# Down projection of a three-product float32r FFN: two of three matmuls joined over a whole PSUM bank, and weight sums moved from Pool to accumulating DMAs

## The chip, the cores and the metric

The kernel runs on one core of one Trainium2 chip, as one program. The metric is the device time of one execution in microseconds (us), as the median of several runs. The profile is that of one execution; its engines are PE (TensorE, matmul; PEld is its weight load), DVE (VectorE), ACT (ScalarE), POOL (GpSimd) and SP (SyncE, which here only issues DMAs).

## The reference

One layer of an encoder for 512 tokens of 2048 features, all in float32: a norm, a combined projection, two mixers, an output projection with residual, then a SwiGLU network (FFN) with residual and a last norm. The change touches the FFN alone, and there the last matrix product, the down projection by `w_down`:

```python
D_MODEL, SEQ, D_FF = 2048, 512, 5632

def reference(x, ..., w_gate_up, w_down, final_norm_w):
    ...                                   # norm, input projection, mixers
    x = x + jnp.einsum('bse,ed->bsd', mixed, w_out[l])
    h2 = _rmsnorm(x, ffn_norm_w[l])
    g, u = jnp.split(jnp.einsum('bsd,df->bsf', h2, w_gate_up[l]), 2, axis=-1)
    x = x + jnp.einsum('bsf,fd->bsd', jax.nn.silu(g) * u, w_down[l])
    return _rmsnorm(x, final_norm_w)
```

## The kernel before

**Numbers.** A float32 operand is split into two float32r parts: `hi`, a copy rounded by ACT (L931 for weights), and `lo`, the rest, by a DVE subtraction (L128, the method `sub`). A product of two such operands is three matmuls into the same PSUM region: hi\*bh, hi\*bl, lo\*bh (L180 to L182, in `mm3`; b is the activation).

**Units.** The FFN's matrix products are cut into units, each by a Winograd scheme with seven products in place of eight. A unit has two blocks of 128 output features as rows, 2048 (in the last block of hidden features 1536) of the summed dimension, and all 512 tokens in two halves of H = 256. It loads two raw weight tiles of 128x2048 (upper: `a11`, `a12`; lower: `a21`, `a22`). Products are taken in the order 1, 2, 4, 5, 6, 3, 7 and called p1 to p7 here. One product is eight tiles of 128 features times three matmuls of 256 columns into the first half of one PSUM bank. A product's activations are its "forms" (sums of quarters of the activation, already split), held in SBUF slots of 128x512 as [bh | bl], 256 columns each.

**Sums of weights.** The scheme needs a21 += a22, a11 -= a21, a12 += a11 and a22 += a11 on the raw tiles (L907 to L923, L128, L131). With the flag `dma` set, three of them are DMAs that accumulate, issued by Pool (L907): the first when the lower tile is loaded, the others ahead of p5's weights. Without it two are adds on Pool (L909), ahead of p4's and p6's weights, and a22 += a11 is a DVE add (L131). The subtraction a11 -= a21 is on DVE in both.

**Evictions.** After p1, p5, p6 and p7 ACT copies 256 columns out of PSUM (L962, L969 are among them), after p2 and p3 and twice after p7 DVE adds 256 columns (L131, L134). In the down projection two results of 128x512 are then added to `x1d` in DRAM by accumulating DMAs issued by Pool (L1015).

**The order.** `Stream` runs the products ("steps") of all units one after another. Units 0 to 43 are gate and up; 44 to 51 and 52 to 59 are the down projection over the first two blocks of hidden features (2048 each), 60 to 67 the last block (1536) with residual and norm. Most units run singly, a unit's p3 and p7 being put behind the next unit's p1 and p2. At the borders of the blocks two units are zipped product by product: 44 with 45, 50 with 51, 52 with 53, 58 with 59, 60 with 61. So a form is wanted twice in a row there, and a pair needs four raw tiles, which are all there are (`RAWB` = 4). A unit's raw tiles are loaded when the splits of p3 and p7 of the unit two before are done.

Weights are split four steps ahead of their product (five `hi` and `lo` buffers). The forms of a block come from `hfd` in DRAM, 56 slots of 256 KB, and take the place of the block before: `reload` (L1319) puts a product's eight loads on SP's queue one to three steps after the last unit of a block has used that product. SP's queue is in order, raw weights and forms together.

Slots of 128x512 for temporaries come from the pool `tp`, nine of them (`TPN`). In gate and up the forms of the result are made in such slots (ACT copy L1187 and DVE subtraction) and stored to `hfd`.

The functions that the change touches, and what calls them:

Of the kernel before, what the change touches and what calls it, by code (L numbers as in the profile page):

```python
# [7 lines left out]
F32 = mybir.dt.float32  # L8
# [7 lines left out]
P = 128  # L16
# [6 lines left out]
B12 = 4  # L23
# [14 lines left out]
# Products, by phase, whose forms are spilled unsplit.  # L38
PLAIN = [(), (1, 2, 4), (), ()]
RAWB, HLB = 4, 5  # L40
SPN, TPN, HPN = 39, 9, 19

# [9 lines left out]
class K:  # L52
# [18 lines left out]

    def bank(self, tag):
        return self.ps.tile([P, T], F32, tag=tag, name=self.nm(tag), bufs=self.banks[tag])
# [21 lines left out]
    def rec_constants(self):  # L95
        """The masks of the recurrence's levels, to DRAM, and the lower bounds."""
# [14 lines left out]
        # Lower bounds: softmax over the layers, its running sum, less its first term.  # L111
# [24 lines left out]
    def split(self, hi, lo, src):  # L136
        """src = hi + lo, each of float32r's twelve bits."""
        self.nc.scalar.copy(hi, src)  # L138
        self.sub(lo, src, hi.bitcast(F32))
# [32 lines left out]
    def weights(self, dram, n=DM, pieces=1):  # L172
        """Chunks of [P, <=QW] of a weight row: loaded, split."""
# [10 lines left out]
    def gemm(self, ws, act, tick=None):  # L184
        """act: pairs of a K tile and its parts, in the order of their use."""
# [10 lines left out]
    def rstd_steps(self, sq, n, tn=T, plus=None, keep=None, over=None, fill=lambda n: None):  # L196
        """From squares summed over all but the partitions: 1/rms as columns, then as rows.

        plus: columns of further sums; keep: takes the columns of these; over: columns that
        the result is divided by.  # L200
        """
# [31 lines left out]
    def stationary(self, Kt, B):  # L233
        """kf in the first halves of blocks of 2B, kb in the second."""
# [5 lines left out]
    def recurrence(self, q, Kt, T1, V, res):  # L240
        """q: slot, Kt: [kf|kb], T1: [ff|fb], V: by token tile. Leaves o (in PSUM) in res."""
# [73 lines left out]
def body(tc, xT, small, wi, wp, wo, wg, wd, out):  # L315
    with ExitStack() as ctx:
# [3 lines left out]
        k.tp = k.pool(ctx, "tp", TPN)  # L320
# [26 lines left out]
        forms, rho = out_proj(k, xT, mhl, wo, x1d, fd)  # L347
        with tc.manual_schedule(engines=by_hand):
# [3 lines left out]
def start(k, xT, wi, wp, vd, zd):  # L352
    """x by features, times the gains, and its forms but t3; its 1/rms.

    Meanwhile v of the first four heads, by tokens, and the rest of the first head.
    """
# [141 lines left out]
def load_b12(k, xT):  # L498
    """The second half of the tokens of the first half of x's features."""
# [10 lines left out]
def conv(k, j, u, y):  # L510
    """y: the taps of channels j on u"""
# [7 lines left out]
def stream(k, hT, F, rest, xT, wp, gd, qd, md, zd):  # L519
    """The gates of all heads, some of the q and most of the conv, by units of two tiles."""  # L520
# [52 lines left out]
    # The step after which t3 makes way for b12.  # L573
# [30 lines left out]
def heads(k, ctx, hT, w0, z0, wi, wp, gd, qd, vd, md):  # L604
# [16 lines left out]
    def segment():  # L621
        """A share of the pending recurrence: it has PARTS steps."""
# [8 lines left out]
    def values_mm(w):  # L631
        """v of two heads, by tokens."""
# [782 lines left out]
```

## Time and profile before

| | |
|---|---|
| median of three runs | 2364.51 us (2364.26 to 2366.21) |
| span of the profiled execution | 2367.5 us |
| PE busy | 2329.9 us, 98% of the span, 17226 matmuls |
| DVE busy | 1752.6 us, 74% |
| ACT busy | 1061.4 us, 45% |
| Pool busy | 342.2 us, 14% |
| gate and up (units 0 to 43) | until about 1900 us |
| down projection of the first two blocks (units 44 to 59) | about 1900 to 2220 us |

The page gives busy times as shares of the span. They are averages over stages; what sets the time of a stage is read from the tables of stretches and from PE's own timeline, in which a gap of PE is followed by the name of what ended it. The profiled span is 3.0 us above the median of the runs.

### The profile page before, as it was taken

What the parts mean: (1) busy time and instruction counts of PE and PEld (TensorE: products, weight loads), DVE (VectorE), ACT (ScalarE), POOL (GpSimd) and SP (SyncE); (2) the same over time, 40 slices, a digit from 0 to 9 for tenths busy, and PEclk for the clock granted to TensorE, in tenths of its full rate; (3) what the DMA queues carried; (4) which work ended last, traced back from release to release, by engine and by line L of the source; (5) the groups of instructions that cost most, each with busy time, mean ns of one, the idle gap of its engine ahead of it and who ended that gap; (6) DMA issues with size and microseconds to landing.
All of it is one profiled execution on the core that took longest, in us unless ns stands there. A gap on an engine that the chain in (4) does not pass through costs nothing.

```text
span 2367.5 us, 42647 instructions
## 1 busy us (share of the span) xinstructions
PE 2329.9 (98%) x17226; PEld 2219.7 (94%) x17226; DVE 1752.6 (74%) x2457; ACT 1061.4 (45%) x1593; POOL 342.2 (14%) x300
## 2 busy tenths in 40 slices
PE   8999999999999999999999999999999989999997
PEld 8999999888888788899999999999999989999997
DVE  8867768766667756687777777777777798777777
ACT  7444445333333333444444445454545544444453
POOL 0231110000000100121111111111111033333210
PEclk9999999999999999999999999999999999999998
DMA  6377776221222455567887878788888884975984
GB/s 232 130 213 203 192 190 221 103 77 66 81 81 72 143 173 205 182 227 219 215 228 204 226 212 238 221 243 220 236 228 230 239 285 129 290 226 138 294 235 135
DMA packets 143684, 454.63 MB, mean 192 GB/s; under 512 B 15744, under 2 KB 31872, under 8 KB 118400
## 3 DMA queue, kind: packets, MB, share of 16 engines
q1 hardware_dynamic: 110528, 349.09, 41.3%
q0 software_dynamic: 30640, 100.68, 22.7%
q8 instruction: 135, 2.21, 0.4%
q10 hardware_dynamic: 2320, 2.15, 0.3%
q14 instruction: 61, 0.50, 0.1%
HBM read 291.75 MB, written 71.50 MB: 153 GB/s over the span
## 4 chain that ended last, share of the span: by engine, by line
PE 91%; DMA 5%; DVE 2%; issue 1%; ACT 1%; POOL 0%; POOLq 0%; SPq 0%; DVEq 0%; ACTq 0%
PE g L180 22%; PE g L181 22%; PE g L182 22%; PE r L180 6%; PE r L182 6%; PE r L181 6%; PE r L268 2%; DMA raw<-wd 1%; PE r L311 1%; DVE lo L128 1%; DMA raw<-wg 1%; DMA s<-fd 1%; DMA s<-hfd 1%; PE r L283 1%; DMA raw<-raw 1%
## 5 line engine op out<-in xcount | busy, mean ns | idle before, releaser
L180 PE MATMUL g<-s,hi 128*128 128x256 f32 (+1 forms) x3912 | 1194.7, 305 | 5.7 <-ACT s L962 4.1
L181 PE MATMUL g<-s,hi 128*128 128x256 f32 (+1 forms) x3912 | 1180.5, 302 | 0.0
L182 PE MATMUL g<-s,lo 128*128 128x256 f32 (+1 forms) x3912 | 1179.8, 302 | 0.0
L128 DVE TENSOR_TENSOR lo<-raw,hi 128x1024 fp32r<-128x1024 f32 (+2 forms) x689 | 869.3, 1268 | 329.8 <-ACT hi L931 236.3
L931 ACT CAST hi<-raw 128x1024 fp32r<-128x1024 f32 (+1 forms) x581 | 597.1, 1028 | 837.6 <-PE g L181 336.1
L180 PEld LDWEIGHTS g<-s,hi 128*128 128x128 f32 x3912 | 749.6, 192 | 34.3 <-ACT s L962 4.9
L181 PEld LDWEIGHTS g<-s,hi 128*128 128x128 f32 x3912 | 749.7, 192 | 27.4 <-issue 3.8
L182 PEld LDWEIGHTS g<-s,lo 128*128 128x128 f32 x3912 | 749.1, 191 | 27.3 <-issue 0.2
L180 PE MATMUL r<-s,hi 128*128 128x256 f32 x1296 | 368.4, 284 | 7.5 <-DVE s L131 7.5
L182 PE MATMUL r<-s,lo 128*128 128x256 f32 x1296 | 368.5, 284 | 3.6 <-DVE lo L128 3.6
L181 PE MATMUL r<-s,hi 128*128 128x256 f32 x1296 | 368.1, 284 | 0.0
L907 POOL DMA_DIRECT2D raw<-raw x173 | 150.9, 986 | 967.9 <-ACT hi L931 779.8
L180 PEld LDWEIGHTS r<-s,hi 128*128 128x128 f32 x1296 | 250.3, 193 | 8.7 <-issue 4.4
L182 PEld LDWEIGHTS r<-s,lo 128*128 128x128 f32 x1296 | 250.2, 193 | 4.2 <-DVE lo L128 4.2
L181 PEld LDWEIGHTS r<-s,hi 128*128 128x128 f32 x1296 | 250.2, 193 | 0.0
L909 POOL TENSOR_TENSOR raw<-raw 128x1024 f32<-128x1024 f32 (+1 forms) x48 | 129.2, 2696 | 506.4 <-DVE s L128 188.6
L134 DVE TENSOR_TENSOR s<-s,s 128x512 f32<-128x512 f32 (+1 forms) x258 | 177.1, 693 | 5.6
L138 ACT CAST hi<-raw 128x1024 fp32r<-128x1024 f32 (+1 forms) x108 | 105.1, 984 | 163.8 <-PE g L181 151.1
L128 DVE TENSOR_TENSOR s<-s,s 128x256 fp32r<-128x256 f32 (+2 forms) x302 | 129.6, 458 | 6.5 <-ACT s L138 5.0
L128 DVE TENSOR_TENSOR raw<-raw,raw 128x1024 f32<-128x1024 f32 (+1 forms) x83 | 105.5, 1271 | 4.2 <-DMA raw<-raw 4.2
L131 DVE TENSOR_TENSOR s<-s,r 128x256 f32<-128x256 f32 x166 | 68.8, 415 | 37.2 <-PE r L182 35.9
L219 POOL TENSOR_TENSOR rc<-ms,mhalf 128x4 f32<-128x4 f32 (+1 forms) x13 | 12.7, 979 | 472.4 <-DVE ms L216 472.4
(138 smaller groups left out, 1617.4 us busy)
## 6 DMA issues: line engine op xcount, KB each, us to landing
raw<-wg SPq DMA_DIRECT2D x88, 1024.0 KB, 5.3
raw<-raw POOLq DMA_DIRECT2D x157, 512.0 KB, 7.0
raw<-wp SPq DMA_DIRECT2D x56, 1024.0 KB, 5.2
hfd<-s SPq DMA_DIRECT2D x130, 256.0 KB, 5.7
s<-hfd SPq DMA_DIRECT2D x130, 256.0 KB, 5.4
raw<-wd SPq DMA_DIRECT2D x32, 1024.0 KB, 5.9
raw<-wo SPq DMA_DIRECT2D x16, 1024.0 KB, 5.3
raw<-wd SPq DMA_DIRECT2D x16, 768.0 KB, 4.9
```

The costliest lines, as they stand in the source:

```text
L128: self.nc.vector.tensor_tensor(out=out, in0=a, in1=b, op=ALU.subtract)
L131: self.nc.vector.tensor_tensor(out=out, in0=a, in1=b, op=ALU.add)
L134: self.nc.vector.tensor_tensor(out=out, in0=a, in1=b, op=ALU.mult)
L138: self.nc.scalar.copy(hi, src)
L180: mm(out, ahi, bhi, start=start, stop=False, **kw)
L181: mm(out, ahi, blo, start=False, stop=False, **kw)
L182: mm(out, alo, bhi, start=False, stop=stop, **kw)
L268: nc.tensor.matmul(ps[:, g * P:(g + 1) * P], kc[:, g * P:(g + 1) * P], vap(Qt, g * P, dims), start=True, stop=True)
L283: nc.tensor.matmul(ps[:, j * 256:(j + 1) * 256], Kt[:, d, s * P:(s + 1) * P], Qt[:, 1 - d, tq:tq + 256], start=True, stop=True)
L907: pool.dma_start(out=out, in_=a, accum_op=ALU.add)
L909: pool.tensor_tensor(out=out, in0=out, in1=a, op=ALU.add)
L931: k.nc.scalar.copy(hi, src)
```

## The change

It has four parts.

1. *Two matmuls in one.* The units 44 to 59 are of a new class `Wide`. The weights `hi` meet the whole slot [bh | bl] in one matmul of 512 columns over a whole bank: hi\*bh lands in the first half, hi\*bl in the second. Then lo\*bh, 256 columns, is added to the second half. The wanted product is the sum of the two halves. So each eviction takes both halves (512 columns) into "pair" tiles of 128x2x2x256, four of them (`DPF`), and at the end of each result one more DVE add of 512 columns joins the halves.
2. *Sums by DMA.* `Down` is built with `dma` set: three accumulating DMAs per unit (L916 after) where Pool's two adds and DVE's add into a22 were.
3. *Stores.* The accumulating store to `x1d` (L1072 after) reads every other 256 columns of a pair tile, so its pieces are 1 KB where they were 2 KB.
4. *Room.* The pool `tp` is closed before the FFN and opened again as `tf` with eight slots instead of nine; the program's scratch for descriptors of DMAs is set to 2048 where the default stood, which gives SBUF room back; a form's entry in `F` holds the whole slot as a third item. Docstrings went, so line numbers move.

The core of the diff:

```diff
+TPF, DPF = 8, 4
+RING = 2048
+    def pair(self):
+        return self.tp.tile([P, 2, 2, H], F32, tag="d", name=self.nm("d"), bufs=DPF)
...
         forms, rho = out_proj(k, xT, mhl, wo, x1d, fd)
+        tctx.close()
+        k.tp = k.pool(tctx, "tf", TPF, side="right", reuse_waits="tile")
...
+class Wide(Unit):
+    def product(self, p, w):
...
+        for j in range(self.nj):
+            s = slice(j * P, (j + 1) * P)
+            f = self.F[FORMS[p], j][2]
+            mm(ps, w[0][:, s], f, start=start and j == 0, stop=False, skip_group_check=True)
+            mm(ps[:, H:], w[1][:, s], f[:, :H], start=False, stop=stop and j == self.nj - 1,
+               skip_group_check=True)
+
+    def post(self, p):
+        k = self.k
+        copy = k.nc.scalar.copy
+        two = lambda ps: vap(ps, 0, [[H, 2], [1, H]])
+        if p == 1:
+            self.G = k.pair()
+            copy(self.G[:, 0], two(self.b))
+        elif p == 2:
+            k.add(self.G[:, 0], self.G[:, 0], two(self.a))
+        elif p == 5:
+            self.W = k.pair()
+            copy(self.W[:, 1], two(self.d))
+        elif p == 6:
+            copy(self.G[:, 1], two(self.b))
+        elif p == 3:
+            G = self.G
+            k.add(G[:, 1], G[:, 1], two(self.d))
+            k.add(G[:, :, 0], G[:, :, 0], G[:, :, 1])
+        elif p == 7:
+            W = self.W
+            copy(W[:, 0], two(self.b))
+            k.add(W[:, 1], W[:, 1], W[:, 0])
+            k.add(W[:, 0], W[:, 0], two(self.e))
+            k.add(W[:, :, 0], W[:, :, 0], W[:, :, 1])
...
-class Down(Unit):
+class Down(Wide):
     def post(self, p, add0, add1):
         super().post(p)
         if p == 7:
-            for out, t in ((add0, self.g), (add1, self.lower())):
-                self.k.nc.gpsimd.dma_start(out=out, in_=t, accum_op=ALU.add)
+            for out, t in ((add0, self.G), (add1, self.W)):
+                self.k.nc.gpsimd.dma_start(out=out, in_=t[:, :, 0], accum_op=ALU.add)
...
-            make.append((lambda b=b, c=c, d=d: Down(k, (wd[d, :, c], wd[d + 8, :, c]), F[1 + b]),
+            make.append((lambda b=b, c=c, d=d: Down(k, (wd[d, :, c], wd[d + 8, :, c]), F[1 + b], True),
...
-    nc = _bacc.Bacc("TRN2", target_bir_lowering=False, num_devices=1)
+    nc = _bacc.Bacc("TRN2", target_bir_lowering=False, num_devices=1,
+                    dynamic_dma_scratch_size=RING)
```

PE, in one product of the first down units. The names are output bank, then form and weight part; `s` is a form's slot. Before:

```order
L180 MATMUL g_2581_20119<-s_2516_19720,hi_2565_19990 128x256
L181 MATMUL g_2581_20119<-s_2516_19720,hi_2565_19990 128x256
L182 MATMUL g_2581_20119<-s_2516_19720,lo_2569_20020 128x256
L180 MATMUL g_2581_20119<-s_2517_19722,hi_2565_19990 128x256
L181 MATMUL g_2581_20119<-s_2517_19722,hi_2565_19990 128x256
L182 MATMUL g_2581_20119<-s_2517_19722,lo_2569_20020 128x256
```

And after:

```order
L1021 MATMUL g_2579_20074<-s_2516_19726,hi_2564_19979 128x512
L1022 MATMUL g_2579_20074<-s_2516_19726,lo_2567_20000 128x256
L1021 MATMUL g_2579_20074<-s_2517_19728,hi_2564_19979 128x512
L1022 MATMUL g_2579_20074<-s_2517_19728,lo_2567_20000 128x256
L1021 MATMUL g_2579_20074<-s_2518_19730,hi_2564_19979 128x512
L1022 MATMUL g_2579_20074<-s_2518_19730,lo_2567_20000 128x256
```

Three instructions per tile became two; the columns per tile, 768, stay the same.

DVE in the first stretch, units 44 and 45 (raw 2504 and 2511 are the upper and lower weights of 44, raw 2508 and 2514 those of 45; `r` is the bank of p2). Before:

```order
L128 TENSOR_TENSOR raw_2504_19595<-raw_2504_19595,raw_2511_19676 128x1024
L128 TENSOR_TENSOR lo_2569_20020<-raw_2511_19676,hi_2565_19990 128x1024
L128 TENSOR_TENSOR raw_2508_19637<-raw_2508_19637,raw_2514_19715 128x1024
L131 TENSOR_TENSOR s_2561_19959<-s_2561_19959,r_2568_19995 128x256
L128 TENSOR_TENSOR lo_2572_20051<-raw_2514_19715,hi_2570_20023 128x1024
L131 TENSOR_TENSOR s_2566_19992<-s_2566_19992,r_2571_20026 128x256
L128 TENSOR_TENSOR lo_2575_20082<-raw_2504_19595,hi_2573_20054 128x1024
L128 TENSOR_TENSOR lo_2578_20112<-raw_2508_19637,hi_2576_20085 128x1024
L131 TENSOR_TENSOR raw_2511_19676<-raw_2511_19676,raw_2504_19595 128x1024
```

And after:

```order
L134 TENSOR_TENSOR raw_2504_19599<-raw_2504_19599,raw_2511_19680 128x1024
L134 TENSOR_TENSOR lo_2567_20000<-raw_2511_19680,hi_2564_19979 128x1024
L134 TENSOR_TENSOR raw_2508_19641<-raw_2508_19641,raw_2514_19720 128x1024
L137 TENSOR_TENSOR d_2561_19955<-d_2561_19955,r_2566_19983 128x512
L134 TENSOR_TENSOR lo_2570_20025<-raw_2514_19720,hi_2568_20005 128x1024
L137 TENSOR_TENSOR d_2565_19981<-d_2565_19981,r_2569_20008 128x512
L134 TENSOR_TENSOR lo_2573_20047<-raw_2504_19599,hi_2571_20027 128x1024
L134 TENSOR_TENSOR lo_2576_20068<-raw_2508_19641,hi_2574_20049 128x1024
L134 TENSOR_TENSOR lo_2580_20091<-raw_2504_19599,hi_2577_20070 128x1024
```

The order stays, with the adds out of PSUM twice as wide and the add into a lower raw tile gone; the two subtractions of raw tiles now follow an accumulating DMA where they followed a Pool add.

Pool around units 52 and 53. Before:

```order
L909 TENSOR_TENSOR raw_2758_21614<-raw_2758_21614 128x1024
L1015 DMA x1d_83<-s_2706_21317 128x512
L1015 DMA x1d_83<-s_2711_21350 128x512
L909 TENSOR_TENSOR raw_2761_21645<-raw_2761_21645 128x1024
L1015 DMA x1d_83<-s_2773_21695 128x512
L1015 DMA x1d_83<-s_2776_21725 128x512
L909 TENSOR_TENSOR raw_2751_21550<-raw_2751_21550 128x1024
L909 TENSOR_TENSOR raw_2755_21583<-raw_2755_21583 128x1024
```

And after:

```order
L916 DMA raw_2752_21216<-raw_2752_21216 128x1024
L1072 DMA x1d_83<-d_2700_20983 256x1x256
L1072 DMA x1d_83<-d_2704_21009 256x1x256
L916 DMA raw_2755_21240<-raw_2755_21240 128x1024
L1072 DMA x1d_83<-d_2745_21171 256x1x256
L1072 DMA x1d_83<-d_2750_21196 256x1x256
L916 DMA raw_2743_21167<-raw_2743_21167 128x1024
L916 DMA raw_2752_21216<-raw_2743_21167 128x1024
L916 DMA raw_2748_21192<-raw_2748_21192 128x1024
L916 DMA raw_2755_21240<-raw_2748_21192 128x1024
```

The two adds per unit are three DMAs, of which the last two stand together; the stores to `x1d` keep their places between them.

## Rows read from the trace of the kernel before

**Rows 1.** The page: busy us, share of span, instructions of each engine.

```profile
PE 2329.9 (98%) x17226; PEld 2219.7 (94%) x17226; DVE 1752.6 (74%) x2457; ACT 1061.4 (45%) x1593; POOL 342.2 (14%) x300
```

**Rows 2.** Stretches, single units: window, us, busy by engine, PEclk, DMA share, GB/s.

```profile
1930.00:2020.00 90.00, 89.93 (x750) 89.72 (x748) 71.14 (x68) 38.87 (x54) 33.66 (x19) 1.00 0.59 171
...
2110.00:2180.00 70.00, 70.00 (x586) 70.00 (x585) 53.06 (x45) 28.35 (x37) 23.34 (x13) 1.00 0.50 133
```

**Rows 3.** The same view: 512-column matmuls of an earlier stage, then 256-column ones.

```profile
900.00:950.00 50.00, 50.00 (x222) 41.39 (x221) 28.20 (x47) 16.55 (x28) 0.00 (x0) 1.00 0.58 198
...
1950.00:2000.00 50.00, 50.00 (x419) 50.00 (x419) 39.67 (x36) 20.54 (x27) 15.60 (x9) 1.00 0.55 136
```

**Rows 4.** PE's timeline, units 44, 45 (start, us; bracket: idle before); the stretch.

```profile
1900.04 0.28 PE L180 MATMUL r<-s,hi 128*128 128x256 f32 x1
...
1902.23 0.39 PE L182 MATMUL r<-s,lo 128*128 128x256 f32 x1 [1.79 <-DVE lo L128]
...
1906.28 0.38 PE L182 MATMUL r<-s,lo 128*128 128x256 f32 x1 [0.91 <-DVE lo L128]
...
1917.42 0.36 PE L180 MATMUL r<-s,hi 128*128 128x256 f32 x1 [4.22 <-DVE s L131]
...
1890.00:1921.00 31.00, 23.02 (x173) 22.04 (x172) 29.58 (x31) 13.63 (x21) 10.70 (x4) 0.95 0.99 375
```

**Rows 5.** Timeline of DVE and of Pool in the same stretch.

```profile
1898.77 3.41 DVE L128 TENSOR_TENSOR lo<-raw,hi 128x1024 fp32r<-128x1024 f32 x1
...
1905.00 1.22 DVE L128 TENSOR_TENSOR lo<-raw,hi 128x1024 fp32r<-128x1024 f32 x1
...
1895.89 5.20 POOL L909 TENSOR_TENSOR raw<-raw 128x1024 f32<-128x1024 f32 x2 [30.96 <-DVE lo L128]
```

**Rows 6.** Stretches with sums by DMA in gate/up, one with a store; Pool's issues.

```profile
1526.00:1535.00 9.00, 9.00 (x78) 9.00 (x77) 6.41 (x11) 4.35 (x6) 1.89 (x3) 1.00 0.93 175
1508.00:1516.00 8.00, 8.00 (x69) 8.00 (x68) 7.22 (x14) 4.09 (x7) 0.86 (x1) 1.00 1.06 227
2133.00:2136.00 3.00, 3.00 (x27) 3.00 (x26) 2.10 (x5) 1.42 (x3) 1.03 (x2) 1.00 0.72 87
...
1525.28 0.86 POOL L907 DMA_DIRECT2D raw<-raw  x1 [16.01 <-ACT hi L931]
1526.45 1.75 POOL L907 DMA_DIRECT2D raw<-raw  x2 [0.30 <-issue]
```

**Rows 7.** Units 50 to 53: SP's reloads, the stretch, PE's begin of 50.

```profile
2029.41 15.06 SPq L1319 DMA_DIRECT2D s<-hfd  x22
...
2054.80 29.68 SPq L1319 DMA_DIRECT2D s<-hfd  x33
...
2029.00:2086.00 57.00, 57.00 (x478) 57.00 (x477) 45.59 (x39) 23.66 (x30) 18.99 (x11) 1.00 1.02 341
...
2020.13 0.39 PE L180 MATMUL g<-s,hi 128*128 128x256 f32 x1 [0.20 <-ACT s L962]
```

**Rows 8.** Units 58 to 61: the stretch and PE's begin of 58.

```profile
2188.00:2241.00 53.00, 53.00 (x444) 53.00 (x444) 38.29 (x39) 21.65 (x31) 17.20 (x11) 1.00 0.97 308
...
2181.83 0.39 PE L180 MATMUL g<-s,hi 128*128 128x256 f32 x1 [0.17 <-ACT s L962]
```

**Rows 9.** Entry into units 42 and 43: chain of waits, and stretch.

```profile
1827.68 6.10 DMA raw<-raw
...
1836.69 8.07 DMA raw<-wg
...
1836.00:1852.00 16.00, 13.70 (x102) 13.49 (x101) 8.97 (x13) 5.96 (x8) 0.86 (x1) 0.89 0.75 223
```

**Rows 10.** Groups of instructions (busy us, mean ns | idle before); ACT's waits.

```profile
L131 DVE TENSOR_TENSOR s<-s,g 128x256 f32<-128x256 f32 x103 | 42.4, 418 | 46.4 <-PE g L182 46.0
...
L131 DVE TENSOR_TENSOR s<-s,s 128x512 f32<-128x512 f32 x62 | 42.5, 685 | 1.0
...
ACT s L962 <- DMA hfd<-s: 2.8, 1, 2.8
```

More of the change, by code (lines that the diff above doesn't have):

```diff
@@ L319, in body @@
         k.sp = k.pool(ctx, "sp", SPN)
-        k.tp = k.pool(ctx, "tp", TPN)
+        tctx = ctx.enter_context(ExitStack())
+        k.tp = k.pool(tctx, "tp", TPN, side="right")
         k.ps = k.pool(ctx, "ps", 1, PSUM)
@@ L831, in form @@
         else:
-            F[name, j] = (f[:, :H], f[:, H:])
+            F[name, j] = (f[:, :H], f[:, H:], f)
     steps = k.rstd_steps(k.ssum, DM, plus=k.xsum)
@@ L946, in product @@
             s = slice(j * P, (j + 1) * P)
-            bh, bl = self.F[FORMS[p], j]
+            bh, bl = self.F[FORMS[p], j][:2]
             k.mm3(ps[:, :H], w[0][:, s], w[1][:, s], bh, bl, start and j == 0,
@@ L991, in post @@
             done(1, s)
+class Wide(Unit):
+    def product(self, p, w):
+        k = self.k
+        mm = k.nc.tensor.matmul
+        bank = {1: "b", 2: "a", 3: "d", 4: "e", 5: "d", 6: "b", 7: "b"}[p]
+        start, stop = p in (1, 2, 4, 5), p in (2, 3, 4, 7)
+        if start:
+            setattr(self, bank, k.bank("g" if bank in "bd" else "r"))
+        ps = getattr(self, bank)
+        for j in range(self.nj):
[5 more added lines that the diff above has]
+    def post(self, p):
+        k = self.k
+        copy = k.nc.scalar.copy
[20 more added lines that the diff above has]
+            k.add(W[:, :, 0], W[:, :, 0], W[:, :, 1])
 class GateUp(Unit):
@@ L1319, in reload @@
                 nc.sync.dma_start(out=f.bitcast(F32), in_=src)
-            F[phase][FORMS[p], j] = (f[:, :H], f[:, H:])
+            F[phase][FORMS[p], j] = (f[:, :H], f[:, H:], f)
     def splits_due(i):
```

## The prediction

> **What bounds the kernel now.** I read the page's engine line first: PE is busy 98% of the span [rows 1]. So time is saved only by fewer or shorter matmuls, or by removing the few waits of PE. Next, the table of stretches over the down projection, to see who could take PE's place. In its single units DMA is busy 0.50 to 0.59, DVE 53 of 70 us and ACT 28 of 70 us [rows 2]. Third, how fast PE issues: 222 matmuls of 512 columns in 50 us are 225.2 ns each, 419 of 256 columns are 119.3 ns each, both at full clock [rows 3]. Each instruction therefore carries about 12 ns beside its columns, and PE follows its instruction count and columns, not what an engine beside it does. Fourth, PE's gaps: in the first stretch of the down projection (units 44 and 45) PE ran 173 matmuls in 31 us where 260 fit, so 10.4 us were lost [rows 4]; units 52, 53 and 60, 61 lost nothing. Last, DMA in those paired stretches, where the forms of the next block are reloaded: it is at 0.97 to 1.02, that is, full [rows 4, 7, 8]. PE is the bound; DMA stands right behind it in three stretches.
>
> **PE's saving.** A triple now takes 3 x 119.3 = 357.9 ns. Afterwards it is one matmul of 512 and one of 256 columns: 225.2 + 119.3 = 344.5 ns. No row shows the two sizes in turn, but both carry the same 12 ns. 16 units x 7 products x 8 tiles = 896 triples, so 896 x 13.4 ns = **-12.0 us**. If only the 12 ns of one instruction went it would be -10.7; I keep -12. A step of eight triples then takes 2.76 us, and a unit of seven 19.3.
>
> **Evictions, on DVE and ACT.** A unit's four adds from PSUM of 0.42 us become six of 0.69 [rows 10]: 1.7 becomes 4.1. DVE loses the add into a22, which has the size of the undisturbed 1.22 us split [rows 5]. It is also freed of Pool: beside a Pool add, that split took 3.41 us instead of 1.22 [rows 5], 2.2 us more, twice per unit. Net 4.1 - 1.7 - 1.2 - 4.4 = -3.2 us per unit of DVE, which was at 76%. ACT's four copies double in width; were all its 28 us doubled, it would still be below 70 [rows 2]. Both lie beside PE, at nothing, except in the first stretch.
>
> **The first stretch (44, 45).** PE's waits there are for DVE: 1.79, twice 0.91, and 4.22 us [rows 4]; DVE is busy 29.6 of 31 us, and Pool's adds stretch its work [rows 5]. Moving the adds off Pool removes what the first of these waits hangs on. But the last wait is for DVE's add of a second product, which frees a bank. In the order it stands behind the subtraction for unit 45, and that now waits for an accumulating DMA. So DVE's stall goes, and DMA is late next.
>
> **The sums' price in DMA.** From 1526 to 1535 only three sums of 512 KB run, at a share of 0.93 over 9 us: 8.4 us, **2.8 us of all sixteen engines each** [rows 6]. 16 units x 3 = 48 sums are 134 us of DMA in about 320 us. Beside other transfers the share reads 1.06 [rows 6], so I divide demands by 1.06. In single units the cover is there: 0.50 x 20 = 10.0 us per unit, plus 8.4, over 1.06 is 17.4 of 19.3 us. I cost them at nothing there. Pool itself issues a DMA in 0.9 us [rows 6] where an add held it over 2 us, so Pool's own queue is no bound.
>
> The Trainium skill, DMA: Bandwidth & Descriptors, section Anatomy of one DMA, fits a Pool-issued transfer as 2.0 us plus bytes over 436 GB/s, of which only the second part moves data. By that, as an estimate, a sum occupies DMA 1.2 us instead of 2.8. The trace disagrees: its sums move 175 GB/s while the share is 0.93 [rows 6].
>
> **The paired stretches, as a ledger** (DMA work before, plus the sums that must land by the pair's last product, against the moment PE wants it).
>
> - *52, 53*: from 2029 to 2086 DMA does 57 x 1.02 = 58.1 us, reloads above all; SP issues 33 in 29.7 us, at DMA's own pace [rows 7]. By the seventh product of unit 53 ten sums come on top (two each of 50 and 51, six of 52 and 53): 28 us. (58.1 + 28) / 1.06 = 81.2, so the work ends at 2110. PE began unit 50 at 2020.1 [rows 7]; 26 steps of 2.76 later, at 2092, it starts the product for which the last forms come, and it wants the last of these 2 us later. **+16**, between 0 (sums and reloads find gaps that the share doesn't show) and +24 (capacity 1.00 instead of 1.06).
> - *44, 45*: 31 x 0.99 = 30.7, plus six sums 16.8, over 1.06 = 44.8: until 1934.8. The third step began at 1900.04 [rows 4]; eleven steps later is 1930.4, plus 2 for the last form: 2 to 4 us late. I take 4 where 10.4 were lost: **-6**, between -10 and +5.
> - *60, 61*: 53 x 0.97 = 51.4, plus four sums 11.2, over 1.06 = 59: until 2247. Unit 58 began at 2181.8 [rows 8]; 14 steps of 2.76, then 12 of 18 matmuls (2.15 us), come to 2246. **+1**, 0 to +5.
>
> **Entries into pairs (50 and 58).** Where gate/up with DMA sums enters a pair, the chain goes sum 6.1 us, split, load 8.1 us, then PE, and from 1836 to 1852 PE ran 102 of 134 matmuls, so 3.8 us were lost, half-rate stretch included [rows 9]. The down projection's entries now lose about 0.3 each and take over that chain: 2 x 3.5 = **+7**, 0 to +8.
>
> **Clock.** In the window just named the granted clock is 0.89 on average: after a long gap PE runs at the lower level for some us, which cost 1.4 of the 3.8 us. For one more long gap (52, 53): **+1.5**.
>
> **Stores to x1d.** They now leave SBUF in pieces of 1 KB, twice as many. No row shows an accumulating transfer with such pieces. One of before takes 3 x 0.72 = 2.2 us [rows 6]. Bounds: nothing (bytes alone count) to 2.2 each (pieces alone count). I take +0.5, near the byte end, because the sums, with pieces twice as large, move bytes at about the pace the store reaches. Six in the ledger of 52, 53: **+3**. At the upper bound a single unit is (18.4 + 4.4) / 1.06 = 21.5 of 19.3 us.
>
> **Moved and freed things.** GateUp's order is unchanged, but its slots go from nine to eight. The longest such wait now is 2.8 us, once [rows 10]; cost 0, with a rival below. The smaller descriptor ring is shown by no row; it could hold Pool back only where the queue is already full.
>
> **Sum**: -12 - 6 + 16 + 1 + 7 + 1.5 + 3 = **+10.5 us**. On the profiled span of 2367.5 that is 2378; the median of the runs, 2364.5, lies 3.0 (0.13%) below that span, and on it the sum gives 2375. I forecast **2376**, own range 2366 to 2392. A measurement of this kernel can tell about 0.2%, 4.7 us, from no change.
>
> **Rivals.**
>
> 1. *Everything hides; PE's gain shows.* For it: reloads are asked for 13 steps ahead, some 37 us, and DVE is relieved. Against: that lead is used up in 52, 53, where DMA already stands at 1.02 for 57 us. Time: -12 - 10 - 1 gives 2341; with half of the first stretch's loss kept, 2347. Chance 0.22.
> 2. *A sum occupies DMA for 1.2 us only*, as that page's rule would have it. 52, 53: (58.1 + 12) / 1.06 ends at 2095, +1; 44, 45: no loss, -10; entries +7: -12 - 10 + 1 + 7 = -14, so 2350. The rows speak against it. Chance 0.05.
> 3. *The two sides cancel.* Part of the lateness in 52, 53 is absorbed (6 instead of 16, 1 KB pieces free): 2362 to 2367, within 0.2%. Chance 0.14.
> 4. *DMA bounds the single units too*, which is slower than before by more than I forecast. Place: units 46 to 49 and 54 to 57. Price: 2.2 us per unit, if the 1 KB pieces double a store; for 8 to 10 units +18 to +22 on the forecast: 2394 to 2398. It decides once a store takes over 1 us more (18.4 + 2 over 1.06 = 19.3). Chance 0.11.
> 5. *Eight slots hold ACT in gate/up*: a cast of a form waits for the store of an older one. At 1.3 us per pair of units (less than the one wait seen) and 21 pairs, up to +27: 2376 to 2400. Chance 0.04.
>
> **How the numbers follow.** Forecast 0.44, rivals 0.22, 0.05, 0.14, 0.11, 0.04. Faster by over 0.2%: rivals 1 and 2, 0.27. Within: rival 3 and the forecast's lowest part, 0.17. Slower: the rest, 0.56. The range 2346 to 2400 takes in rival 1's upper half; it leaves out its lower half and the upper tail, not quite 0.2.
>
> **What would show it.** PE: 1792 matmuls in place of 2688, and some 290 in 50 us in a single unit (16 per 2.76). DVE's 128x1024 splits without 3.4 us ones before unit 60. DMA at 0.87 to 0.95 in 46 to 49, and full from 2029 to about 2110. A PE gap of over 10 us in 52, 53, ended by a reload or a sum, with a half-rate stretch behind it. Wrong: no gap in 52, 53 (rival 1 or 2, told apart by the share during three lone sums); gaps in every single unit (rival 4); ACT waits for hfd stores in gate/up (rival 5).

## The result and the profile after

| | predicted | measured |
|---|---|---|
| median | 2376 us (2346 to 2400) | 2404.9 us (2399.4 to 2408.7, 4 runs) |
| before, the same comparison | | 2364.4 us (2363.2 to 2366.2, 4 runs) |
| ratio | 1.005 | 1.0161, 95% interval 1.0146 to 1.0177 |

The changed kernel is slower, as forecast, but by 40 us in place of 11.5; the time lies above the range. The profiled execution of the changed kernel has a span of 2404.8 us, 37.3 more than before.

The page of the changed kernel: engines, and two queues of part 3 (packets, MB, share of sixteen engines' span). They answer to [rows 1].

```profile
PE 2340.4 (97%) x16330; PEld 2182.9 (91%) x16330; DVE 1724.9 (72%) x2473; ACT 1072.8 (45%) x1593; POOL 307.3 (13%) x316
...
q1 hardware_dynamic: 110528, 349.09, 40.4%
q0 software_dynamic: 41648, 125.85, 27.8%
```

PE issues 896 matmuls less. Pool's queue q0 takes 27.8% of 2404.8 us, 668 us; before its row was

```profile
q0 software_dynamic: 30640, 100.68, 22.7%
```

which is 537 us of 2367.5. The 48 sums (and the smaller pieces of the stores) brought 131 us of DMA, 2.7 us each; in e2 below, which has the sums alone, it is 27.7% of 2394.7 us, 126 us more than before and 2.6 us each. The price of a sum was right; what it does at its place was not.

Where PE stood still: its timeline in the changed kernel, the ten gaps over 1.5 us of units 44 to 61 (start, us; in brackets the idle time before, and what ended it).

```profile
1908.44 0.76 PE L1021 MATMUL r<-s,hi 128*128 128x512 f32 x1 [2.38 <-DVE d L137]
...
1936.39 0.80 PE L1021 MATMUL g<-s,hi 128*128 128x512 f32 x1 [4.00 <-ACT d L1038]
...
1953.83 0.77 PE L1021 MATMUL r<-s,hi 128*128 128x512 f32 x1 [6.21 <-DVE d L137]
...
2026.63 0.50 PE L1021 MATMUL g<-s,hi 128*128 128x512 f32 x1 [2.30 <-ACT d L1036]
...
2072.45 0.50 PE L1021 MATMUL g<-s,hi 128*128 128x512 f32 x1 [1.65 <-ACT d L1038]
...
2095.23 0.77 PE L1021 MATMUL r<-s,hi 128*128 128x512 f32 x1 [5.55 <-DVE d L137]
...
2124.79 0.49 PE L1021 MATMUL g<-s,hi 128*128 128x512 f32 x1 [3.21 <-ACT d L1038]
...
2137.38 0.77 PE L1021 MATMUL r<-s,hi 128*128 128x512 f32 x1 [4.00 <-DVE d L137]
...
2210.41 0.50 PE L1021 MATMUL g<-s,hi 128*128 128x512 f32 x1 [2.19 <-ACT d L1036]
...
2274.84 0.56 PE L186 MATMUL r<-s,hi 128*128 128x256 f32 x1 [4.09 <-DVE s L137]
```

None of these names a DMA. PE waits for a bank, and the ACT copy or DVE add that empties the bank stands, in its engine's order, behind a cast or a subtraction that waits for a DMA. One must follow the chain one step back to see the cause.

From the start of unit 44 to the start of unit 62 the kernel before needs 364.0 us, in which PE is idle for 8.2 us and stands at the lower clock for 3.4; the changed kernel needs 405.3, with 37.6 us of idle time and 44.4 us at the lower clock (worked out from the records of all matmuls and of the granted clock). So of the 41.3 us, 29.4 are idle time. PE's own saving was 6 us, so some 18 are matmuls at the lower clock of 1.2 GHz, to which PE fell in or after gaps.

The same kernel, table of stretches (window, us, busy by engine, PEclk, DMA share, GB/s); it answers to [rows 2, 4, 7].

```profile
1885.00:1905.00 20.00, 18.57 (x117) 16.37 (x116) 16.47 (x25) 11.09 (x18) 1.74 (x2) 1.00 1.03 352
1905.00:1930.00 25.00, 22.62 (x123) 19.53 (x122) 14.12 (x18) 9.71 (x14) 3.50 (x4) 0.93 1.06 316
1930.00:1943.00 13.00, 8.99 (x37) 7.49 (x36) 6.75 (x11) 4.54 (x7) 2.13 (x3) 0.74 1.02 398
1943.00:1951.00 8.00, 4.62 (x27) 3.78 (x26) 1.12 (x2) 0.29 (x1) 1.89 (x2) 1.00 1.12 262
...
1960.00:2000.00 40.00, 40.00 (x228) 34.70 (x227) 28.21 (x31) 18.78 (x23) 8.57 (x9) 1.00 0.96 218
2040.00:2062.00 22.00, 22.00 (x126) 19.07 (x125) 12.68 (x13) 9.89 (x12) 3.53 (x4) 1.00 1.05 277
2066.00:2118.00 52.00, 44.50 (x233) 36.79 (x232) 26.56 (x28) 18.05 (x22) 9.69 (x10) 0.93 1.07 319
```

In the single units (1960 to 2000) DMA stands at 0.96 and PE loses nothing. In the paired stretches DMA is at 1.02 to 1.12 throughout, and PE loses time in all of them but the one from 2040 to 2062. DVE, which was busy 29.6 of 31 us in the first stretch [rows 4], is idle 40% of the four windows up to 1951; it is no longer what ends last.

How far PE lags behind the kernel before at the start of some products (44p7 is product p7 of unit 44), both counted from the start of unit 44 (worked out from the starts of each product's first matmul in the profiled executions; minus is ahead):

```
us                                44p7   47p1   49p6   50p1   52p1   55p1   57p6   58p1   60p1   62p1
changed kernel                    -6.8   +8.4   +7.3  +10.8  +12.0  +30.6  +29.5  +32.9  +32.4  +41.3
e1  joined matmuls, Pool sums     +1.3   +3.3   +2.2   +6.0   +4.5   +4.5   +3.5   +6.9   +5.4   +5.4
e2  sums by DMA alone             -6.3   +6.4   +6.4   +7.0   +7.3  +22.5  +22.5  +26.7  +26.7  +32.4
e4  as changed, DMA in 44, 45     -6.1   +4.7   +3.7   +6.9   +5.4   +5.4   +4.4   +7.5   +6.0   +6.0
e6  short sums by DMA             -6.3   -6.3   -6.3   -6.7   -6.7   -6.7   -6.7   -6.7   -6.7   -6.7
e11 half sums by DMA              -7.0   +1.5   +1.5   +1.6   +1.6   +4.0   +4.0   +3.6   +3.6   +3.6
e7  joined matmuls, DVE sums      -4.1   -4.5   -5.6   -6.2   -6.9   -7.9   -9.0   -9.6  -10.3  -10.4
e14 joined, DMA in singles        -3.1   -3.5   -4.5   -3.9   -4.6   -5.6   -6.7   -7.4   -8.9   -8.9
e12 as e7, evictions first        -7.9   -8.3   -9.4   -9.2  -10.7  -12.8  -14.9  -14.4  -15.1  -15.1
e13 as changed, evictions first   -6.6   +6.4   +5.4   +5.2   +4.4  +22.1  +20.0  +23.1  +21.8  +24.7
```

The first row tells the story by place. The first pair gains 6.8 us and then gives back 15 by unit 47; the entries into 50 and 58 cost 3.5 each; the stretch of 52 to 54 costs 18.6; the one of 60 and 61 costs 8.9; between them the lag falls by 1.1 us per 20 products.

### The profile page after: what moved, and what is told of

Read it like the earlier page. It is cut to its first block, busy times and chain, and to the rows that moved or that the text cites. A ratio compares the mean times of both kernels' runs of the same rounds, so it can differ in the third digit from the quotient of the medians.

```text
span 2404.8 us, 40897 instructions
## 1 busy us (share of the span) xinstructions
PE 2340.4 (97%) x16330; PEld 2182.9 (91%) x16330; DVE 1724.9 (72%) x2473; ACT 1072.8 (45%) x1593; POOL 307.3 (13%) x316
## 3 DMA queue, kind: packets, MB, share of 16 engines
q0 software_dynamic: 41648, 125.85, 27.8%
## 4 chain that ended last, share of the span: by engine, by line
PE 45%; DMA 8%; DVE 2%; issue 2%; ACT 1%; SPq 0%; POOL 0%; POOLq 0%; ACTq 0%; DVEq 0%
PE g L186 9%; PE g L187 9%; PE g L188 9%; DMA s<-hfd 4%; PE r L186 4%; PE r L188 4%; PE r L187 4%; PE g L1021 3%; DMA raw<-wd 2%; DMA raw<-raw 2%; PE g L1022 2%; PE r L1021 1%; DVE lo L134 1%; DMA raw<-wg 1%; PE r L1022 1%
## 5 line engine op out<-in xcount | busy, mean ns | idle before, releaser
L134 DVE TENSOR_TENSOR lo<-raw,hi 128x1024 fp32r<-128x1024 f32 (+2 forms) x689 | 823.4, 1202 | 367.5 <-ACT hi L940 282.3
L186 PE MATMUL g<-s,hi 128*128 128x256 f32 (+1 forms) x3272 | 1013.1, 310 | 4.6 <-ACT s L971 3.3
L187 PE MATMUL g<-s,hi 128*128 128x256 f32 (+1 forms) x3272 | 999.1, 305 | 0.0
L188 PE MATMUL g<-s,lo 128*128 128x256 f32 (+1 forms) x3272 | 998.6, 305 | 0.0
L186 PEld LDWEIGHTS g<-s,hi 128*128 128x128 f32 x3272 | 626.7, 192 | 32.4 <-ACT s L971 3.7
L187 PEld LDWEIGHTS g<-s,hi 128*128 128x128 f32 x3272 | 626.7, 192 | 27.3 <-issue 3.6
L916 POOL DMA_DIRECT2D raw<-raw x221 | 194.2, 988 | 1179.0 <-ACT hi L940 715.6
L186 PE MATMUL r<-s,hi 128*128 128x256 f32 x1040 | 296.4, 285 | 6.1 <-DVE s L137 6.0
L188 PE MATMUL r<-s,lo 128*128 128x256 f32 x1040 | 296.0, 285 | 1.5 <-DVE lo L134 1.5
L187 PE MATMUL r<-s,hi 128*128 128x256 f32 x1040 | 295.8, 284 | 0.0
L1021 PE MATMUL g<-s,hi 128*128 128x512 f32 x640 | 234.0, 407 | 13.7 <-ACT d L1038 8.9
L186 PEld LDWEIGHTS r<-s,hi 128*128 128x128 f32 x1040 | 201.1, 193 | 7.4 <-issue 4.5
L188 PEld LDWEIGHTS r<-s,lo 128*128 128x128 f32 x1040 | 201.2, 193 | 1.9 <-DVE lo L134 1.9
L187 PEld LDWEIGHTS r<-s,hi 128*128 128x128 f32 x1040 | 201.3, 194 | 0.0
L1022 PE MATMUL g<-s,lo 128*128 128x256 f32 x640 | 182.2, 285 | 0.0
L1021 PEld LDWEIGHTS g<-s,hi 128*128 128x128 f32 x640 | 123.4, 193 | 47.5 <-ACT d L1038 10.2
```

The costliest lines, as they stand in the source:

```text
L134: self.nc.vector.tensor_tensor(out=out, in0=a, in1=b, op=ALU.subtract)
L186: mm(out, ahi, bhi, start=start, stop=False, **kw)
L187: mm(out, ahi, blo, start=False, stop=False, **kw)
L188: mm(out, alo, bhi, start=False, stop=stop, **kw)
L916: pool.dma_start(out=out, in_=a, accum_op=ALU.add)
L1021: mm(ps, w[0][:, s], f, start=start and j == 0, stop=False, skip_group_check=True)
```

## The experiments

Two theories stood first. **S**: the sums by DMA cost the time. **W**: the joined matmuls cost it, by wider evictions, four pair tiles and stores in smaller pieces.

**Taking the parts apart (e1 to e4).** The joined matmuls alone:

```diff
-    ... Down(k, (wd[d, :, c], wd[d + 8, :, c]), F[1 + b], True),
+    ... Down(k, (wd[d, :, c], wd[d + 8, :, c]), F[1 + b]),
```

> The joined matmuls alone: as the changed kernel, but the sums of weights of the down units are on Pool and DVE again, as before. Theory S (the sums by DMA cost the time: they fill DMA and stand between the load of the raw weights and the split): the gaps of PE in units 46, 50, 54 and 58 go, units 44 and 45 lose some 10 to 14 us as before, PE saves about 6 us (112 steps of 2.83 in place of 2.88 us): 2355 to 2362 us. Theory W (the joined matmuls cost it: wider evictions, only four pair tiles, stores in pieces of 1 KB that hold them): the gaps at 46, 52 and 54 stay, 2390 to 2400 us.

Measured: 2368.0 us, ratio 1.0006 (0.9994 to 1.0019). That is far from W, but also above what S gave it. The first pair gains nothing here: Pool's adds are back. The gaps at 46 to 54 shrink to a few us. The two entries stay: 3.8 us from 49p6 to 50p1 and 3.4 from 57p6 to 58p1, without any sum by DMA in a down unit. Timeline of e1 ahead of the entry, Pool, DVE and ACT:

```profile
2005.91 3.42 POOL L918 TENSOR_TENSOR raw<-raw 128x1024 f32<-128x1024 f32 x1 [1.66 <-DMA raw<-wd]
...
2006.99 3.42 DVE L137 TENSOR_TENSOR raw<-raw,raw 128x1024 f32<-128x1024 f32 x1
2010.34 0.67 DVE L137 TENSOR_TENSOR d<-d,g 128x512 f32<-128x512 f32 x1
2011.05 0.69 DVE L137 TENSOR_TENSOR d<-d 128x512 f32<-128x512 f32 x1
2011.66 1.22 DVE L134 TENSOR_TENSOR lo<-raw,hi 128x1024 fp32r<-128x1024 f32 x1
...
2019.17 1.04 ACT L940 CAST hi<-raw 128x1024 fp32r<-128x1024 f32 x1 [5.70 <-DMA raw<-wd]
```

The split at 2011.66 frees a raw tile and starts the load of unit 50's weights, for which ACT then waits 5.70 us, and the evictions behind it too. DVE reaches that split late, since a Pool add held its add for 3.42 us and the evictions ahead of the split are now 0.67 and 0.69 where one of 0.41 stood. So wider evictions are not free there: they are in the chain that ends at the load, together with Pool's add. Without Pool's adds (e7 below) the entries lose nothing, with the same evictions.

The sums by DMA alone:

```diff
-    ... Down(k, (wd[d, :, c], wd[d + 8, :, c]), F[1 + b]),
+    ... Down(k, (wd[d, :, c], wd[d + 8, :, c]), F[1 + b], True),
```

> The sums by DMA alone: the kernel before with the three accumulating DMAs per down unit, all else unchanged (matmuls of 256 columns, stores of 2 KB pieces, nine slots). Theory S: the gaps of the changed kernel at 46, 50, 52, 54 and 58 are here too, and PE's 6 us are missing: 2400 to 2412 us. Theory W: the first stretch loses less and nothing else changes: 2354 to 2364 us.

Measured: 2397.4 us, ratio 1.0133 (1.0108 to 1.0159). 31 of the 40 us are here, 2.6 us below the range of S and at the same places as in the changed kernel (table), but for the entry into 50, which loses 0.6 us: S holds. Chain of waits of e2 at unit 46 (start, us, what):

```profile
1922.67 5.37 DMA s<-hfd
...
1928.11 10.56 DMA raw<-wd
...
1939.23 8.04 DMA raw<-raw
...
1947.35 1.05 ACT hi L931
1948.39 0.28 ACT s L969
```

A late reload, then the raw weights of unit 46, then the sum on them, then the cast, and only then the eviction that gives PE its bank.

The room alone (eight slots, pool opened again, small scratch for descriptors):

```diff
+TPF = 8
+RING = 2048
...
+        tctx.close()
+        k.tp = k.pool(tctx, "tf", TPF, side="right", reuse_waits="tile")
```

> The room alone: the kernel before with eight slots in place of nine from the FFN on, in the pool as the changed kernel opens it, and the small scratch for descriptors. Theories S and W: no change, 2362 to 2367 us. My fifth rival (eight slots hold ACT in gate and up): 2370 us or more, with waits of ACT for stores to hfd.

Measured: 2364.7 us, ratio 0.9998 (0.9988 to 1.0007). No price; my fifth rival falls.

The sums by DMA in the first pair alone, the other units on Pool:

```diff
-    ... F[1 + b], True),
+    ... F[1 + b], b == 0 and d < 2),
```

> The changed kernel with the sums by DMA in units 44 and 45 alone; the other fourteen down units sum on Pool and DVE as before. Theory S, with the chain load, sum, split as what stops units 46 and 54: the first pair saves its 8 to 10 us and gives back 0 to 5 of it where the raw weights of 46 land behind the reloads; no gap by a sum after that: 2346 to 2358 us. Theory W: the gaps at 52 and 54 stay: 2380 to 2395 us.

Measured: 2371.0 us, ratio 1.0022 (1.0008 to 1.0036). Both theories missed. Units 44 and 45 gain 6.1 us (8 to 10 expected), but at 47 they have given back 10.8, though unit 46 has no sum by DMA here. Its timeline of SP's queue and of ACT:

```profile
1885.39 43.53 SPq L1376 DMA_DIRECT2D s<-hfd  x33
1929.30 0.33 SPq L166 DMA_DIRECT2D raw<-wd  x1
...
1936.43 1.04 ACT L940 CAST hi<-raw 128x1024 fp32r<-128x1024 f32 x1 [9.53 <-DMA raw<-wd]
```

SP needs 43.5 us to issue 33 reloads, and only then comes to the raw weights of 46. In the kernel before it was

```profile
1886.17 29.90 SPq L1319 DMA_DIRECT2D s<-hfd  x34
...
1925.43 0.33 SPq L160 DMA_DIRECT2D raw<-wd  x1
```

There the reloads were out at 1916.1, and the upper weights of 46 left at 1925.4, when the split that frees their raw tile was done. In e4 that split is done at 1917.3, and the queue holds these weights for another 12 us. The six sums of the pair are 6 x 2.7 = 16 us of DMA; 13.6 of them appear in SP's time. The trace also shows how a full DMA lengthens this queue: SP's DMAs take eight semaphores in turn, and most of them are issued at the moment when the DMA eight places ahead of them lands (25 of 37 from 1895 to 1945 in the changed kernel, within 0.12 us). So the first theory on the spot (load, sum, split in a row) is only the second half of the cause: the weights themselves land late. e4 doesn't show the weights quite alone: behind them stand a Pool add and a DVE subtraction that takes 3.31 us beside it.

**Bytes or the wait for a sum (e5, e6, e11).** In e5 the kernel before keeps its sums, and as many bytes go into scratch tiles that nobody uses:

```diff
+class Down(Unit):
+    def extra(self, a):
+        x = self.k.scratch
+        x.append(x.pop(0))
+        self.k.nc.gpsimd.dma_start(out=x[0], in_=a, accum_op=ALU.add)
```

> The bytes of the sums without their place in the chain: the kernel before, with its sums on Pool and DVE, and besides three accumulating DMAs of 512 KB per down unit, issued where the sums by DMA stand, into scratch tiles whose content nobody uses. If it is the bytes (they fill DMA, so reloads and raw weights land late): 2385 to 2400 us, SP needs some 44 us for the 33 reloads at units 44 and 45 where it needed 30. If it is the wait for each sum: 2364 to 2370 us.

Measured: 2419.2 us, ratio 1.0229 (1.0213 to 1.0246). It is above both ranges and slower than the whole change, but not for the bytes alone: the two entries lose 12 to 13 us each, because the idle transfers read the raw tiles and stand in Pool's queue ahead of its adds, so the tiles come free late. What it shows cleanly is the queue of SP in the first stretch:

```profile
1881.60 40.03 SPq L1340 DMA_DIRECT2D s<-hfd  x34
```

40 us for 34 reloads, with nobody waiting for a sum. The upper weights of 46 were not held by the queue here, though: they left at 1925.2, when their tile came free, and at 47p1 the run is 0.6 us behind the kernel before. By itself the run is inconclusive. The next one takes the bytes away and leaves the wait:

```diff
+            q = slice(0, 64 if self.short else out.shape[-1])
+            pool.dma_start(out=out[:, q], in_=a[:, q], accum_op=ALU.add)
```

> The place in the chain without the bytes: the kernel with the sums by DMA alone, but each sum of a down unit moves only the first 64 of 1024 columns (the rest of the sum is left out, so the output is not the reference's). If it is the bytes: the time falls below before, since DVE no longer suffers from Pool and DMA has its old load: 2354 to 2362 us. If it is the wait for each sum, some 2 to 3 us of latency however small: 2375 to 2390 us.

Measured: 2358.9 us, ratio 0.9968 (0.9957 to 0.9979): faster than before. The gain at 44 and 45 stays through all stretches (table). It is the bytes: the sums stand in the same chain, and the last four of the first pair still take 5.5 to 6.1 us each from issue to landing (in the changed kernel 7.9 to 14.7). With half of them:

> The kernel with the sums by DMA alone, each sum moving 512 of 1024 columns (the other half of the sum is left out, so the output is not the reference's). With 64 columns it took 2358.9 us, with all 1024 it took 2397.4. If the loss begins where DMA is full (24 us less DMA work in each eight units than with whole sums): 2362 to 2376 us, below the middle of 2378. If each sum costs by its duration wherever it stands: 2376 to 2381.

Measured: 2367.4 us, ratio 1.0003 (0.9990 to 1.0016). 64, 512 and 1024 columns give 2359, 2367 and 2397 us: the first half of the bytes costs 8.5 us, the second half 30. A cost in proportion to the bytes of each sum would be even; this one sets in late. That fits a DMA that runs out of room, but also a wait that has some slack; e14 below tells the two apart, with whole sums in the same chain where DMA has room.

**Sums without DMA and without Pool (e7, e8).**

```diff
 class Down(Wide):
+    def sum(self, out, a):
+        self.k.add(out, out, a)
```

> The changed kernel with the sums of the down units on DVE in place of DMA. A Pool add stretches a DVE split beside it from 1.2 to 3.4 us, so three adds of 1.2 us on DVE itself should cost DVE less than before. If bytes and Pool's collisions make all of the loss: the first stretch loses 6 to 9 us instead of 13.6, the entries at 49 and 57 lose 1 to 2 us instead of 4 each, PE's 6 us stay: 2350 to 2358 us. If the wider evictions on DVE are too much for it (the entries still lose 4 each, gaps at 44 to 46): 2362 to 2372 us.

Measured: 2353.9 us, ratio 0.9954 (0.9938 to 0.9971). The kernel before with the same edit:

> The kernel before with all sums of the down units on DVE, nothing else changed. If Pool's collisions with DVE make the 13.6 us of the first stretch: it loses 6 to 9 us and the time is 2356 to 2361 us. If what comes late there is DMA (reloads, then the raw weights of unit 46), the gain at 44 and 45 is given back at 46: 2362 to 2366 us.

Measured: 2361.4 us, ratio 0.9982 (0.9973 to 0.9991), with 4.1 us gained in the first pair and kept; it lies just above the first of its two ranges. So part of the stall there was Pool's, and with the DMA work of the kernel before, reloads and weights come in time for a PE that is 4 us earlier. The entries of e7 lose nothing. The Trainium skill, SBUF — State Buffer, section Terms, says that DVE and GpSimd hold a shared port pair exclusively for a whole instruction and the loser blocks. The traces agree: beside Pool an add of DVE took 3.42 us, where one alone took 1.22, and it ended 1.08 us after Pool's add did (e1, 2006.99 and 2005.91).

**The order of evictions (e12, e13).** In both, from unit 44 on, a product's evictions come ahead of the next split in ACT's and DVE's order:

```diff
-            self.wsplit(i + L)
-            if i:
-                self.post(i - 1)
+            if i and n >= 44:
+                self.post(i - 1)
+            self.wsplit(i + L)
+            if i and n < 44:
+                self.post(i - 1)
```

> The joined matmuls with the sums on DVE, and from unit 44 on ACT and DVE take the evictions of a product ahead of the next weights' split, not behind it. If the banks that PE waits for in unit 45 are late only by their place in DVE's order: 2349 to 2353 us. If DVE's whole work bounds the first stretch, or the splits become late in turn: 2353 to 2362 us.

Measured, on top of e7: 2348.5 us, ratio 0.9925 (0.9910 to 0.9939). That is the fastest version, 18.7 us below the kernel before in the same comparison. Timeline of PE of e12 in the first pair:

```profile
1902.33 0.39 PE L1022 MATMUL r<-s,lo 128*128 128x256 f32 x1 [1.80 <-DVE lo L134]
...
1908.70 0.47 PE L1021 MATMUL r<-s,hi 128*128 128x512 f32 x1 [0.69 <-DVE d L137]
```

and the engines on its page:

```profile
PE 2317.8 (99%) x16330; PEld 2168.2 (92%) x16330; DVE 1773.3 (76%) x2521; ACT 1076.8 (46%) x1593; POOL 265.1 (11%) x268
```

The wait of 4.22 us for a bank in [rows 4] is 0.69 here, and PE is busy 99% of the span. By the table the order itself is worth 4 us (-4.5 to -8.3 at 47p1); of the rest, part is pace, of which the last section tells. The same order on the changed kernel itself, sums by DMA kept:

> The changed kernel, sums by DMA, with the evictions of a product ahead of the next weights' split on ACT and DVE from unit 44 on. If the weights themselves come late because DMA is full, the order helps little: 2392 to 2403 us. If most of PE's gaps are banks whose evictions stand behind a cast that waits for a load or a sum, though the weights of the next four steps are there: 2365 to 2385 us.

Measured: 2390.7 us, ratio 1.0085 (1.0061 to 1.0108). That lies between its two ranges. Of the 40 us, the order gives back 14 (by the two ratios 18); some 20 us above before stay. PE's waits of e13 from 1885 to 2290 (us in total, times, longest):

```profile
PE g L1022 <- DVE lo L134: 7.8, 4, 3.3
PE r L1021 <- DVE d L137: 5.0, 2, 3.6
PE r L1022 <- DVE lo L134: 4.4, 3, 1.8
PE g L1021 <- DMA s<-hfd: 3.9, 3, 2.2
```

Now PE waits mostly for the split weights and for reloads by name; 5.0 us of waits for a bank are left in this list. The larger part of the loss is thus lateness of data; the smaller part is evictions queued behind a waiting cast.

**Where the sums are hidden (e14).** Sums by DMA in units 46 to 49 and 54 to 57, on DVE in the pairs:

```diff
-    ... F[1 + b]),
+    ... F[1 + b], 2 <= d <= 5),
```

> The joined matmuls with the sums by DMA in the single units 46 to 49 and 54 to 57 alone, on DVE in the pairs. If the sums have cover in single units, as the prediction has it: 2351 to 2360 us, as with all sums on DVE. If the first single unit behind a pair is the place that is late, its raw weights standing behind the reloads and its sum behind the weights: 2362 to 2380 us, with gaps at 46 and 54 alone.

Measured: 2356.1 us, ratio 0.9950 (0.9931 to 0.9970). A stretch of it:

```profile
1960.00:2010.00 50.00, 50.00 (x285) 43.36 (x284) 33.74 (x37) 22.12 (x26) 11.66 (x12) 1.00 0.93 216
```

PE is busy all of it at a DMA share of 0.93, and there is no gap at 46 or 54 either; one gap of 1.01 us stands at the entry into 50. In single units the sums are free; in the pairs, and for the unit behind a pair, they are not (e2).

**Pieces of the stores (e9, e10).** The pair tiles laid out so that a result is contiguous:

```diff
-            copy(self.G[:, 0], two(self.b))
+            copy(self.G[:, :, 0], two(self.b))
...
-                self.k.nc.gpsimd.dma_start(out=out, in_=t[:, :, 0], accum_op=ALU.add)
+                self.k.nc.gpsimd.dma_start(out=out, in_=t[:, 0].rearrange("p a b -> p (a b)"), accum_op=ALU.add)
```

> The changed kernel with the pair tiles laid out so that a result is contiguous: the stores to x1d leave in pieces of 2 KB again, all else as in the changed kernel. If the smaller pieces have a price in DMA (landing 7.5 us in the changed kernel, 4.4 before) and so hold the pair tiles for which ACT waits at unit 52: 2390 to 2401 us. If a store costs by its bytes alone: 2402 to 2408 us.

Measured: 2400.2 us, ratio 1.0143 (1.0128 to 1.0158), whose interval overlaps that of the changed kernel; a price of a few us is possible and not shown. On DMA the smaller pieces took 6 us more in all 32 stores (668 of the changed kernel against 27.6% of 2400.9), 0.2 us each. In its profiled execution e9 also ran 65 of its 112 steps at the faster of PE's two paces (last section), the changed kernel 9.

> The joined matmuls with the sums on DVE and with stores of 2 KB pieces. DMA has room there, so the pieces should matter little by either theory: 2350 to 2355 us.

Measured: 2355.0 us (2346.3 to 2355.2), ratio 0.9943 (0.9923 to 0.9962), like e7.

## Why the prediction was wrong

*What held.* PE was the bound, and DMA stood right behind it in the paired stretches. A sum costs 2.7 us of DMA (2.8 foreseen), not 1.2. The single units hide the sums: the share is 0.96 in the changed kernel and 0.93 in e14, where 0.87 to 0.95 was foreseen. Rival 5 has no price. Rival 4 came near the time, but not by its mechanism: units 47, 48, 55 and 56 lost nothing, and the gaps at 46, 54 and the ends of 49 and 57 hang on the pairs beside them.

*Right in size, in part by luck.* Units 52 and 53 with 54 behind them cost 18.6 us from 52p1 to 55p1, where +16, +1.5 and +3 were in the sum. But the forecast let PE wait for the last forms, in one gap of over 10 us. There were three: 5.55 us at 53p4, for a bank whose add stood behind a subtraction that waited for a sum (issued at 2079.0, landed at 2093.2); 3.21 at 53p7, behind the cast of unit 54's weights; and 4.00 at 54p4, behind the sum on these weights. SP issued the weights of 54 only behind the reloads:

```profile
2116.03 7.08 DMA raw<-wd
```

Ahead of the first of the three gaps ACT also waited 7.61 us for a store that held a pair tile; e2, which has no pair tiles, has a gap of 4.16 at the same place. The stores' +0.5 each measured as 0.2 (e9). By its own numbers the ledger's upper bound here is +21, not +24, and that of rival 5 is 2403, not 2400; neither decides anything.

*The step that failed, first stretch (-6 foreseen).* The gain came: -6.8 at 44p7. Then 15.2 us were lost up to 47p1. My ledger closed with "plus 2 for the last form". It asked when the last reload lands, and left out what stands behind the reloads in SP's in-order queue: the raw weights of units 46 and 47. Chain of waits of the changed kernel:

```profile
1910.75 13.98 DMA s<-hfd
1924.80 5.26 DMA s<-hfd
1930.13 11.21 DMA raw<-wd
...
1941.98 8.63 DMA raw<-raw
1950.71 1.04 ACT hi L940
1951.76 0.49 ACT d L1045
```

All reloads but one had landed by 1932.0, within the ledger's end of 1934.8. The upper weights of 46 landed at 1934.7, the lower ones at 1941, the sum on these at 1951, and PE, 6.8 us ahead of before, stood still for the first and for the sum (4.00 and 6.21 us). The split that frees the upper weights' tile was done at 1916.3; SP issued them at 1927.5, behind the reloads. In the kernel before PE's wait for DVE came first, and the queue was empty when the tile came free: a gain on PE ahead of a full queue is not kept. e4 shows the weights' part with Pool's sums behind them, e6 that all of it goes with the bytes.

*The same step, 60 and 61 (+1 foreseen).* From 60p1 to 62p1 the lag grows by 8.9 us. There too the ledger counted the forms alone. In the changed kernel the raw weights of 60 and 61 are issued late, between reloads, and what follows falls together. Timelines of SP, Pool and DVE:

```profile
2245.47 0.33 SPq L166 DMA_DIRECT2D raw<-wd  x1
...
2246.82 2.11 SPq L166 DMA_DIRECT2D raw<-wd  x2
...
2260.29 2.44 POOL L918 TENSOR_TENSOR raw<-raw 128x768 f32<-128x768 f32 x1 [0.69 <-DVE d L137]
...
2260.94 2.34 DVE L137 TENSOR_TENSOR d<-d 128x512 f32<-128x512 f32 x1
```

These two units still sum on Pool, and one of the new joins of halves, 0.69 us alone, takes 2.34 beside it. The first stretch's collision of DVE and Pool has moved here, onto more DVE work. The joins are the smaller part: e2, which has none, loses 5.7 of the 8.9 us here. In e7 nothing is lost here, with the same Pool adds but weights that come in time.

*Evictions "beside PE, at nothing".* True of the busy time, wrong at the entries. The +7 there was right in size: 3.5 and 3.4. In the changed kernel the chain is sum, then load (7.97 and 7.64 us ahead of 50), as foreseen. But the sums alone (e2) lose 0.6 and 4.2 there, and e1, with wider evictions and Pool's adds and no sum by DMA, loses 3.8 and 3.4: the cost had two causes, one behind the other, and the forecast named one.

*Clock (+1.5 foreseen for one more gap).* There are twelve gaps over 0.4 us where four were, and the lower clock took some 18 us, 1.5 per gap. [rows 9] had shown 1.4 per gap; their number was wrong, and this follows from the steps above.

*PE's saving (-12 foreseen).* 6 us in the changed kernel: most steps last 2.83 us, not 2.76, where 2.88 stood before. At the faster of two paces, which e10 held for 105 of 112 steps, a step lasts 2.77 and the saving is the 12 us foreseen; the last section tells of it.

Of the 29 us by which the forecast missed, the first stretch is about 15, units 60 and 61 are 8, PE's saving 6; the lower clock is counted in the stretches in which it fell.

## What to carry to other kernels

Where an in-order queue carries two kinds of loads, a ledger of bytes has to close with the last thing in that queue that somebody waits for, not with the last of the kind that one is thinking of. Work moved from an engine to DMA is free only in stretches where DMA has room, and a mean share over stages hides those where it has none; here the same sums cost nothing in single units and some 30 us in the pairs and right behind them. When PE waits for a bank, look at what the evicting engine has in front of the eviction: putting evictions ahead of casts that may wait was worth 4 us with the sums on DVE and 14 to 18 us with sums by DMA.

## What the hardware showed that was not expected

PE has two paces for the same pair of matmuls, 512 and 256 columns in turn, at the full granted clock. Two stretches, first e7, then e10:

```profile
1960.00:2000.00 40.00, 40.00 (x228) 34.68 (x227) 34.60 (x36) 18.60 (x23) 4.37 (x4) 1.00 0.51 132
```

```profile
1960.00:2000.00 40.00, 40.00 (x233) 35.28 (x232) 34.84 (x37) 19.09 (x23) 3.46 (x4) 1.00 0.50 138
```

In e10 each pair takes 347 ns (230 and 117 between starts); in e7 they run through a cycle of three pairs, with 512 columns at 232, 236 and 240 ns, 353 ns per pair. In the records looked at, the pace changes only where PE is held up, if only for 48 ns, and then holds until the next time: the changed kernel ran at 347 from 44p5 to 45p6 and at 353 from 46p6 to 49p5; e12 changed from 353 to 347 between 49p6 and 50p1, where it had a gap of 0.53 us. Over 112 steps this is some 6 us, and it explains why PE's saving was half of that foreseen. It doesn't explain the spread among runs: the profiled execution of e10 ran at the faster pace and still took 2355.1 us, near the top of 2346.3 to 2355.2, and the kernel before, which has no such pairs, spreads as much (2362.3 to 2372.6 in the same comparison). What sets the pace after a gap was not found.
